# A hybrid decoder block on one core: three made-ahead operand kinds stored unsplit, a final norm computed by positions, and a reordered end

## The chip, the cores and the metric

The kernel runs on one core of one Trainium2 chip. The metric is the device time of one execution in microseconds, taken as the median of several runs.

The five engines have the names that the profile gives them. PE is the matmul engine, and PEld its weight loads. DVE, ACT and POOL are the three elementwise engines. SP issues every DMA of this kernel.

## The reference

One layer of a decoder block on 2048 positions with 1024 channels:

```python
h = rmsnorm(x, norm1_g)
proj = h @ w_in                      # queries, keys, values, gates, conv inputs
o_gla = silu(p_g) * rmsnorm(gated_linear_attention(q, k, v, log_a))
o_conv = c_b * causal_depthwise_conv(c_c * c_h)
x = x + concat(o_gla, o_conv) @ w_out
h2 = rmsnorm(x, norm2_g)
x = x + (silu(h2 @ w_ffn_gate) * (h2 @ w_ffn_up)) @ w_ffn_down
return rmsnorm(x, norm_f_g)
```

`rmsnorm` divides a position's 1024 channels by the root of their mean square plus 1e-6, and multiplies by a gain per channel.

## The kernel before

**Layout.** Activations lie transposed: channels on the 128 partitions, positions along the row. The 2048 positions are four blocks of 512. A half is two blocks (`j` is 0 or 1), and the input projection, the output projection and the feed-forward part each run over half 0 and then half 1.

**Products.** A float32 operand is written as a sum of two reduced-precision (`fp32r`) tiles, `hi` and `lo`, by `split` (lines 145 to 147): ACT copies with rounding (line 146), DVE subtracts (line 147). Each product is three matmuls, hi·hi, hi·lo and lo·hi (lines 359 to 361). A `unit` (line 365 on) multiplies a 2x2 block matrix of weights with a 2x2 block matrix of activations in seven products in place of eight; the activation operands are called, in the order of use, B11, T1, T2, B21, T3, B22 and T4, with four tiles each. A tile of operands holds `hi` beside `lo`, 128 x 1024 words. The pool `opp` has 28 of them.

**Operands made ahead.** While half 0 is multiplied, a generator that is stepped between the products makes the operands of half 1 (`combine`, line 266 on) and puts them into DRAM. `h1_ahead` does so for the input projection: it splits each operand and stores `hi` and `lo` with two DMAs. `h2_ahead` does so for the feed-forward part, through `store_split` (one DMA of 512 KB from a pool of three buffers `so`). When half 1 begins, `load_pairs` and `load_h2` load 28 operands, already split, into `opp`.

**Final norm of half 0.** `finish_later` is stepped while half 1's feed-forward part runs. For each block `j` it sums the squares by channels, and `psum_rstd` (line 167) multiplies the sums by a matrix of ones (line 171), which leaves the total of each position on all partitions, 128 x 512. `finish_rstd` (lines 175 to 180) then makes the inverse root: ACT logarithm (line 177) and exponential (line 178), and DVE steps on 128 x 512 tiles (lines 179 and 156 to 158). Line 975 scales.

**The end.** `last_unit` computes the last two channel tiles of half 1 in four groups of 18 matmuls, in the order (j, r) = (0,0), (0,1), (1,0), (1,1). After each group line 1019 adds on DVE, line 1021 squares on ACT, and line 988 applies the gain on ACT. `norm(0)` stands after the group (1,0), `norm(1)` after (1,1): two matmuls with ones (lines 993 and 994), `finish_rstd`, and a copy of the result for POOL (line 996). `scale` (line 1002) then multiplies the eight tiles of one `j`, six on DVE and two on POOL, and stores each. The built program has on DVE, one after the other, the six scales of j = 0, the last add (line 1019), the norm of j = 1, and its six scales. On PE the group (1,1) follows the two matmuls of `norm(0)` directly.

**What sets the order.** Each engine works off its own list in order. The lists come from a scheduler that simulates the whole program when it is built, so an edit can move instructions far from it; `tc.issue_after(x)` keeps what follows behind `x` in that simulation. A DMA waits in SP's one list until its source or its destination is ready.

Of the kernel before, what the change touches and what calls it, by code (L numbers as in the profile page):

```python
# [10 lines left out]
F32 = mybir.dt.float32  # L11
F32R = mybir.dt.float32r
U32 = mybir.dt.uint32
AF = mybir.ActivationFunctionType
ALU = mybir.AluOpType
PSUM = bass.MemoryType.PSUM
# [2 lines left out]
P = 128  # L19
D = 1024  # L20
SEQ = 2048
PB = 512
NB = SEQ // PB
KD = D // P
PT = PB // P
# [6 lines left out]
EPS = 1e-6  # L32


PRODUCTS = [
    ("A11", "B11"), ("S1", "T1"), ("S2", "T2"), ("A12", "B21"),
    ("S3", "T3"), ("S4", "B22"), ("A22", "T4"),
]
# [2 lines left out]
LATER = ("B21", "T3", "B22", "T4")  # L41


C_G1, C_G2, C_GF, C_BG, C_GN, C_CW = 0, 8, 16, 24, 26, 27
N_SMALL = 39

# [2 lines left out]
def tile_hymba_block(ctx, tc, x, xt, win, wa, wgu, wout, wffn, wdown, wdown_first, small, out):  # L49
    nc = tc.nc  # L50
    act, dve, pool, pe = nc.scalar, nc.vector, nc.gpsimd, nc.tensor

    def pool_of(name, bufs, **kw):
        return ctx.enter_context(tc.tile_pool(name=name, bufs=bufs, **kw))

    const = pool_of("const", 1)
    opp = pool_of("opp", 28)
# [3 lines left out]
    tiny = pool_of("tiny", 2)  # L61
    ps = pool_of("ps", 8, space=PSUM)
    dram = pool_of("dram", 1, space=DRAM)

    mixing = ExitStack()
    mixer = mixing.enter_context(tc.tile_pool(name="mixer", bufs=1))
# [1 line left out]
    bx = [mixing.enter_context(tc.tile_pool(name="bx", bufs=11)), None]  # L68


    ident = mixer.tile([P, P], F32, name="ident")
    make_identity(nc, ident)
    ones = const.tile([P, P], F32, name="ones")
    dve.memset(ones[:], 1.0)
# [3 lines left out]
        out=mask[:], in_=mask[:], compare_op=ALU.is_ge, fill=0.0, base=0,  # L78
        pattern=[[0, 2], [1, P]], channel_multiplier=-1,
    )  # L80
    one_t = ones[:, 0:1]
# [16 lines left out]
    def scratch(name, n):  # L98
# [16 lines left out]
        for half in range(2)  # L115
    ]
    s_h2 = {n: [dram.tile([P, PB], F32, name=f"sf{n}_{k}") for k in range(4)] for n in LATER}
    s_h2p = {
        n: [dram.tile([P, 2, PB], F32, name=f"sh{n}_{k}") for k in range(4)] for _, n in PRODUCTS
    }  # L120
    s_h1 = {
        n: [dram.tile([P, 2, PB], F32, name=f"si{n}_{k}") for k in range(4)] for _, n in PRODUCTS
    }

    def col(c):
# [2 lines left out]
    def bank(name="mm"):  # L128
        return ps.tile([P, PB], F32, name=name, tag="mm")
# [4 lines left out]
    def bt(name, shape=(P, PB)):  # L134
        return bx[0].tile(list(shape), F32, name=name, tag="b")

    def load(dst, src):
        return nc.sync.dma_start(dst, src)

    def store(dst, src):  # L140
        return nc.sync.dma_start(dst, src)

    last_hi, raw_loads = [], []

    def split(src, hi, lo):
        last_hi[:] = [act.activation(hi, src, AF.Copy)]  # L146
        return dve.tensor_tensor(lo, src, hi.bitcast(F32), ALU.subtract)  # L147
# [20 lines left out]
    def psum_rstd(ssq, n):  # L168

        tot, rb = bank("tot"), bank("rb_ps")  # L170
        pe.matmul(tot[:], ones[:], ssq[:], start=True, stop=True)
        finish_rstd(ssq, tot, n, rb)
        return rb

    def finish_rstd(v, tot, n, rb=None):
        l, y0 = bt("l"), bt("y0")
        act.activation(l[:], tot[:], AF.Ln, bias=eps[:], scale=1.0 / n)
        act.activation(y0[:], l[:], AF.Exp, scale=-0.5)
        dve.tensor_scalar(v[:], tot[:], 1.0 / n, EPS, ALU.mult, ALU.add)
        newton((v if rb is None else rb)[:], v[:], l[:], y0[:])  # L180
# [38 lines left out]
    def no_operands():  # L219
        return {b: [] for _, b in PRODUCTS}  # L220
# [233 lines left out]
    rbs, raws, first_weights, last_load, rows, squares = {}, {}, {}, [], {}, {}  # L454
# [54 lines left out]
    def h1_ahead():  # L509

        def put(n, k, h):
            hi, lo = [bx[0].tile([P, PB], F32R, name=e, tag="b") for e in ("hi", "lo")]
            split(h[:], hi[:], lo[:])
            for e, y in enumerate((hi, lo)):
                store(s_h1[n][k][:, e, :], y[:].bitcast(F32))

        yield from combine(lambda k, j: xt[2 + j, :, k, :], C_G1, (rbs[2], rbs[3]), put)

    def load_pairs(src):
        ops = no_operands()  # L520
        for _, n in PRODUCTS:
            ops[n] = [load_pair(p) for p in src[n]]
        return ops

    def load_pair(src):
        o = opp.tile([P, 2, PB], F32R, name="op", tag="op")
        load(o[:].bitcast(F32), src[:])
        return o
# [143 lines left out]
    def gla_scores(b, t, kq, kt, v, g):  # L672
# [174 lines left out]
    def h2_ahead(ssq):  # L847


        rb = []  # L850
        for j in range(2):
            for _ in range(2):
                yield
            rb.append(psum_rstd(ssq[j], D))

        def put(n, k, h):
            store_split(s_h2p[n][k], h)

        yield from combine(lambda k, j: s_x1[2 + j][k][:], C_G2, rb, put)

    def load_h2():
        ops, loads = no_operands(), raw_loads[-2]
        for _, n in PRODUCTS:
            for k in range(4):
                o = opp.tile([P, 2, PB], F32R, name="op", tag="op")
                with tc.issue_after(loads.ins):
                    load(o[:].bitcast(F32), s_h2p[n][k][:])
                ops[n].append(o)
        return ops

# [88 lines left out]
    def finish_later(half):  # L959

        for j in range(2):
            ssq = tiny.tile([P, PB], F32, name="ssx0", tag="ssx0", bufs=1)
            for d in range(KD):
                y = bt("y")
                load(y[:], s_x1[2 * half + j][d][:])
                yield
                sum_squares(ssq, y[:], d == 0)
            yield
            act.preload_act_table_set("natural_log_exp_and_others")
            rb = psum_rstd(ssq, D)  # L970
            for d in range(KD):
                y = bt("y")
                load(y[:], s_x1[2 * half + j][d][:])
                yield
                dve.scalar_tensor_tensor(y[:], y[:], col(C_GF + d), rb[:], ALU.mult, ALU.mult)
                store(out[2 * half + j, :, d, :], y[:])

    def last_unit(src, ops, b12, y, ssq):


        raw = raw_weights(src)
        w = [weight_quarter(raw[:, i, :]) for i in (0, 1, 3, 2)]
        columns = (ops["B11"], ops["B21"]), (b12, ops["B22"])
        with tc.issue_after(last_hi[0].ins):
            act.preload_act_table_set("natural_log_exp_and_others")

        def gain(d, j):
            act.activation(y[d, j], y[d, j], AF.Copy, scale=col(C_GF + d))

        def norm(j, q):  # L990

            tot, rb = bank("tot"), bank("rb")
            pe.matmul(tot[:], ones[:], ssq[j][:], start=True, stop=False)
            pe.matmul(tot[:], ones[:], q[:], start=False, stop=True)
            finish_rstd(ssq[j], tot, D, rb)
            act.activation(ssq[j][:], rb[:], AF.Copy)
            return rb

        def scale(j, rb):
            for d in range(KD):  # L1000
                eng, by = (pool, ssq[j]) if d in (2, 5) else (dve, rb)
                eng.tensor_tensor(y[d, j], y[d, j], by[:], ALU.mult)
                store(out[2 + j, :, d, :], y[d, j])

        for d in range(KD - 2):
            for j in range(2):
                gain(d, j)
        q, rbs = {}, []
        for j in range(2):
            for r in range(2):  # L1010
                o = bank()
                with ExitStack() as stack:
                    if j or r:
                        stack.enter_context(tc.issue_after(done.ins))
                    for i in range(2):
                        for k in range(len(b12)):
                            done = product_step(o, w[2 * r + i], columns[j][i], k, i == 0)
                yy = y[KD - 2 + r, j]
                dve.tensor_tensor(yy, o[:], yy, ALU.add)
                q[j] = tt("q")  # L1020
                act.activation(q[j][:], yy, AF.Square)
                gain(KD - 2 + r, j)
                if not r:
                    pool.tensor_tensor(ssq[j][:], ssq[j][:], q[j][:], ALU.add)
                if j and not r:
                    rbs.append(norm(0, q[0]))
        rbs.append(norm(1, q[1]))
        for j in range(2):
            scale(j, rbs[j])


    act.preload_act_table_set("natural_log_exp_and_others")
# [3 lines left out]
    ops, first, differences = build_h()  # L1036
# [9 lines left out]
    ops = load_pairs(s_h1)  # L1046
# [122 lines left out]
```

## Time and profile before

| What | Value |
|---|---|
| median of 3 runs | 2122.82 us (2122.73 to 2124.79) |
| profiled execution | 2120.33 us |
| its span, first to last instruction | 2118.6 us |
| PE busy share | 96% |
| moved by DMA | 470.74 MB |
| granted matmul clock, mean | 0.989 |

The span is what the views of the trace divide into stages; 1.7 us of the profiled execution lie outside it. In a row of a timeline the first number is the start in microseconds from the span's start and the second the duration; the brackets name how long the engine was idle before and what ended it. In a row of stages each engine has its busy time and its instructions, and PEclk is the granted clock of the matmul engine.

### The profile page before, as it was taken

To read this page: it belongs to the slowest core of one execution; us is meant where nothing else is said; L and a number is where in the kernel's file an instruction comes from. 1 tells how busy PE (TensorE), PEld (TensorE's weight loads), DVE (VectorE), ACT (ScalarE), POOL (GpSimd) and SP (SyncE) were. 2 spreads that over 40 slices of the span, in tenths; PEclk is the share of its full clock that TensorE was granted. 3 is DMA by queue.
4 is the path that set the end of the run, shared out by engine and by line. 5 is a ranking of instruction groups with operands and counts; after the bars stand their busy time and mean duration, and the time that the engine had idled before them with its cause. 6 is when DMAs were issued, how large, how long until landed. Compare 5 with 4: busy or idle time off the path is not lost.

```text
span 2118.6 us, 26920 instructions
## 1 busy us (share of the span) xinstructions
PE 2038.3 (96%) x9133; PEld 1651.9 (78%) x9133; DVE 1412.8 (67%) x1983; ACT 1014.8 (48%) x1997; POOL 973.8 (46%) x703
## 2 busy tenths in 40 slices
PE   6999999999999999999999999999999989999996
PEld 4777787887888887778888878787888878877774
DVE  7668775548754696887887565555776766665554
ACT  5555444656543345544545453333554554543344
POOL 3435322222102364555564348764635544436774
PEclk9999999999999999999999999999999999999998
DMA  7349586433586882655655687697455535587662
GB/s 277 125 150 317 184 328 225 137 110 123 181 310 211 335 286 91 232 220 185 232 190 204 229 331 269 236 340 312 150 206 185 200 138 189 181 345 279 268 268 110
DMA packets 190971, 470.74 MB, mean 222 GB/s; under 512 B 20016, under 2 KB 65264, under 8 KB 181232
## 3 DMA queue, kind: packets, MB, share of 16 engines
q1 hardware_dynamic: 190832, 469.01, 60.8%
q8 instruction: 72, 1.18, 0.2%
q14 instruction: 67, 0.55, 0.1%
HBM read 300.63 MB, written 168.30 MB: 221 GB/s over the span
## 4 chain that ended last, share of the span: by engine, by line
PE 78%; DVE 8%; DMA 6%; issue 3%; ACT 2%; POOL 2%; SPq 0%; DVEq 0%; ACTq 0%; POOLq 0%
PE mm L359 22%; PE mm L361 22%; PE mm L360 22%; PE mm L777 2%; PE mm L778 2%; PE mm L780 2%; DVE wq L147 2%; DVE so L147 1%; DMA op<-shT 1%; DMA raw<-in_wffn_dram 1%; DMA raw<-in_wdown_dram 1%; PE a_ps L541 1%; DVE op L147 1%; ACT wq L146 1%; DMA raw<-in_win_dram 1%
## 5 line engine op out<-in xcount | busy, mean ns | idle before, releaser
L359 PE MATMUL mm<-op,wq 128*128 128x512 f32 x2499 | 983.0, 395 | 27.0 <-ACT c L379 10.7
L361 PE MATMUL mm<-op,wq 128*128 128x512 f32 x2499 | 968.3, 393 | 15.2 <-DVE wq L147 14.2
L360 PE MATMUL mm<-op,wq 128*128 128x512 f32 x2499 | 977.6, 391 | 0.0
L147 DVE TENSOR_TENSOR wq<-raw,wq 128x512 fp32r<-128x512 f32 (+2 forms) x626 | 523.3, 843 | 338.6 <-ACT wq L146 336.3
L146 ACT ACTIVATE wq<-raw 128x512 fp32r<-128x512 f32 (+2 forms) x626 | 363.9, 587 | 563.1 <-PE mm L361 407.0
L359 PEld LDWEIGHTS mm<-op,wq 128*128 128x128 f32 x2499 | 471.7, 189 | 141.8 <-ACT c L379 14.8
L361 PEld LDWEIGHTS mm<-op,wq 128*128 128x128 f32 x2499 | 471.5, 189 | 127.9 <-DVE wq L147 29.0
L360 PEld LDWEIGHTS mm<-op,wq 128*128 128x128 f32 x2499 | 472.0, 189 | 97.2 <-issue 1.0
L344 POOL TENSOR_TENSOR raw<-s,raw 128x512 f32<-128x512 f32 (+2 forms) x97 | 128.3, 1323 | 441.7 <-DVE wq L147 421.6
L383 DVE TENSOR_TENSOR c<-mm,c 128x512 f32<-128x512 f32 x267 | 182.9, 685 | 98.4 <-PE mm L361 94.7
L342 POOL TENSOR_TENSOR s<-raw 128x512 f32<-128x512 f32 (+2 forms) x97 | 130.0, 1340 | 206.7 <-DMA raw<-in_wffn_dram 84.8
L349 POOL TENSOR_TENSOR raw<-raw 128x512 f32<-128x512 f32 (+2 forms) x97 | 125.1, 1290 | 139.6 <-DVE wq L147 132.4
L379 ACT ACTIVATE c<-mm 128x512 f32<-128x512 f32 x267 | 154.7, 585 | 39.8 <-PE mm L361 37.4
L759 POOL TENSOR_TENSOR ssx<-ssx,q 128x512 f32<-128x512 f32 x52 | 76.1, 1476 | 155.4 <-ACT q L758 155.2
L343 POOL TENSOR_TENSOR raw<-raw 128x512 f32<-128x512 f32 (+2 forms) x97 | 137.4, 1416 | 4.1
L948 POOL TENSOR_TENSOR y<-c,y 128x512 f32<-128x512 f32 x66 | 98.7, 1498 | 49.0 <-DVE c L383 48.7
L147 DVE TENSOR_TENSOR so<-t,so 128x512 fp32r<-128x512 f32 x100 | 91.0, 916 | 23.6 <-ACT so L146 23.0
L146 ACT ACTIVATE wq<-s 128x512 fp32r<-128x512 f32 (+2 forms) x97 | 56.8, 586 | 95.4 <-PE mm L361 88.6
L777 PE MATMUL mm<-op,wq 128*128 128x512 f32 x256 | 100.9, 395 | 0.0
L778 PE MATMUL mm<-op,wq 128*128 128x512 f32 x256 | 99.8, 390 | 0.0
L147 DVE TENSOR_TENSOR wq<-s,wq 128x512 fp32r<-128x512 f32 (+2 forms) x97 | 85.0, 876 | 15.7 <-ACT wq L146 15.1
L146 ACT ACTIVATE so<-t 128x512 fp32r<-128x512 f32 x100 | 62.3, 626 | 39.2 <-DMA sa_B<-so 14.6
(175 smaller groups left out, 1884.4 us busy)
## 6 DMA issues: line engine op xcount, KB each, us to landing
raw<-in_wffn_dram SPq DMA_DIRECT2D x44, 1024.0 KB, 5.5
sa_T<-so SPq DMA_DIRECT2D x88, 512.0 KB, 5.0
op<-sa_T SPq DMA_DIRECT2D x88, 512.0 KB, 8.7
sa_B<-so SPq DMA_DIRECT2D x69, 512.0 KB, 3.4
op<-sa_B SPq DMA_DIRECT2D x69, 512.0 KB, 9.1
raw<-in_win_dram SPq DMA_DIRECT2D x23, 1024.0 KB, 5.3
raw<-in_wdown_dram SPq DMA_DIRECT2D x24, 768.0 KB, 6.2
sx<-y SPq DMA_DIRECT2D x48, 256.0 KB, 3.2
```

Source lines behind the costliest of these rows:

```text
L146: last_hi[:] = [act.activation(hi, src, AF.Copy)]
L147: return dve.tensor_tensor(lo, src, hi.bitcast(F32), ALU.subtract)
L342: pool.tensor_tensor(s1, a21, a22, ALU.add)
L343: pool.tensor_tensor(a21, a11, a21, ALU.subtract)
L344: pool.tensor_tensor(a11, s1, a11, ALU.subtract)
L359: pe.matmul(o[:], wh, xh, start=first and k == 0, stop=False, skip_group_check=True)
L360: pe.matmul(o[:], wh, xl, start=False, stop=False, skip_group_check=True)
L361: return pe.matmul(o[:], wl, xh, start=False, stop=k == n - 1, skip_group_check=True)
L379: act.activation(t[:], o[:], AF.Copy)
L383: dve.tensor_tensor(t[:], o[:], t[:], ALU.add)
L777: pe.matmul(o[e, j][:], wh, m[:, 0, :], start=k == 0, stop=False)
L778: pe.matmul(o[e, j][:], wh, m[:, 1, :], start=False, stop=False)
```

## The change

1. **Stored whole.** T3, B22 and T4 (12 of the 28 operands) are stored by `h1_ahead` and by `h2_ahead` as they are, 256 KB each, without a split. `load_whole` loads such an operand into the second half of its `opp` tile and splits it there, so ACT's copy and DVE's subtraction are done at the loading.
2. **The norm by positions.** `position_rstd` replaces the norm in `finish_later` and in `last_unit`. The squares are the stationary side of matmuls with one column of ones, four (or eight) per block, so the totals stand as 128 x 4: one position on each partition. DVE alone makes the inverse root, from an integer first guess and three Newton steps: twelve instructions on 128 x 4 tiles. A copy spreads it to 128 x 512, and four transposes put it on all partitions; in `last_unit` four more write a second copy for ACT and POOL. `ident` moves to the pool that lives to the end, and the loads of ACT's function table in `finish_later` and `last_unit` go.
3. **The end.** The last add (line 1019) goes ahead of the scales of j = 0. POOL scales three tiles of j = 0 (2, 5, 6); DVE scales tiles 0 and 1 behind the last add, and tiles 3, 4 and 7 behind the copy `rep` of `norm(1)`.

```diff
+WHOLE = ("T3", "B22", "T4")
...
+    def position_rstd(n, *sums, into=()):
+        s, rb = bank("rs"), bank("rb_ps")
+        tot, v, l = [s[:, i * PT : (i + 1) * PT] for i in range(3)]
+        y = tiny.tile([P, PT], F32, name="py", tag="py")[:]
+        for t in range(PT):
+            for i, ssq in enumerate(sums):
+                pe.matmul(
+                    tot[:, t : t + 1], ssq[:, t * P : (t + 1) * P], one_t, start=i == 0,
+                    stop=i == len(sums) - 1,
+                )
+        dve.tensor_scalar(v, tot, 1.0 / n, EPS, ALU.mult, ALU.add)
+        li = l.bitcast(I32)
+        dve.tensor_scalar(li, v.bitcast(I32), 1, None, ALU.arith_shift_right)
+        dve.tensor_scalar(y.bitcast(I32), li, -1, 0x5F3759DF, ALU.mult, ALU.add)
+        for _ in range(3):
+            dve.tensor_tensor(l, v, y, ALU.mult)
+            dve.scalar_tensor_tensor(l, l, -0.5, y, ALU.mult, ALU.mult)
+            dve.scalar_tensor_tensor(y, l, 1.5, y, ALU.add, ALU.mult)
+        rep = bt("rep", (P, PT, P))
+        last_rep[:] = [
+            dve.tensor_copy(rep[:], y.rearrange("p (t c) -> p t c", c=1).to_broadcast([P, PT, P]))
+        ]
+        for dst in (rb, *into):
+            for t in range(PT):
+                pe.transpose(dst[:, t * P : (t + 1) * P], rep[:, t, :], ident[:])
+        return rb
...
         def put(n, k, h):
+            if n in WHOLE:
+                store(s_h1[n][k][:], h[:])
+                return
...
+    def load_whole(src):
+        o = opp.tile([P, 2, PB], F32R, name="op", tag="op")
+        load(o[:, 1, :].bitcast(F32), src[:])
+        split(o[:, 1, :].bitcast(F32), o[:, 0, :], o[:, 1, :])
+        return o
...
         def put(n, k, h):
-            store_split(s_h2p[n][k], h)
+            if n in WHOLE:
+                store(s_h2p[n][k][:], h[:])
+            else:
+                store_split(s_h2p[n][k], h)
...
-            act.preload_act_table_set("natural_log_exp_and_others")
-            rb = psum_rstd(ssq, D)
+            rb = position_rstd(D, ssq)
...
-            tot, rb = bank("tot"), bank("rb")
-            pe.matmul(tot[:], ones[:], ssq[j][:], start=True, stop=False)
-            pe.matmul(tot[:], ones[:], q[:], start=False, stop=True)
-            finish_rstd(ssq[j], tot, D, rb)
-            act.activation(ssq[j][:], rb[:], AF.Copy)
+            copied = bank("rb_ps")
+            rb = position_rstd(D, ssq[j], q, into=[copied])
+            act.activation(ssq[j][:], copied[:], AF.Copy)
             return rb
...
                 if j and not r:
-                    rbs.append(norm(0, q[0]))
-        rbs.append(norm(1, q[1]))
-        for j in range(2):
-            scale(j, rbs[j])
+                    rb = norm(0, q[0])
+                    for d in (2, 5, 6):
+                        scale(0, d, None)
+        for d in (0, 1):
+            with tc.issue_after(added.ins):
+                scale(0, d, rb)
+        rb1 = norm(1, q[1])
+        for d in (3, 4, 7):
+            with tc.issue_after(last_rep[0].ins):
+                scale(0, d, rb)
+        for d in range(KD):
+            scale(1, d, None if d in (2, 5) else rb1)
```

In the built program of the changed kernel, PE has the eight column matmuls and the eight transposes of `norm(0)` ahead of the 18 matmuls of the group (1,1). On DVE the last add follows the copy `rep` of `norm(0)`, then two scales, the chain of `norm(1)`, three scales of j = 0, and the six of j = 1. In `finish_later`, 24 matmuls stand on PE between the last column matmul and the first transpose for the first block, and 12 for the second. At the start of each half 1, the twelve splits of `load_whole` stand in the lists of ACT and DVE among the weight splits of the first two units.

More of the change, by code (lines that the diff above doesn't have):

```diff
@@ L13 @@
 U32 = mybir.dt.uint32
+I32 = mybir.dt.int32
 AF = mybir.ActivationFunctionType
@@ L68, in tile_hymba_block @@
     bx = [mixing.enter_context(tc.tile_pool(name="bx", bufs=11)), None]
-    ident = mixer.tile([P, P], F32, name="ident")
+    ident = const.tile([P, P], F32, name="ident")
     make_identity(nc, ident)
@@ L117, in tile_hymba_block, with made_ahead @@
     s_h2 = {n: [dram.tile([P, PB], F32, name=f"sf{n}_{k}") for k in range(4)] for n in LATER}
+    def made_ahead(name, n):
+        return dram.tile([P, PB] if n in WHOLE else [P, 2, PB], F32, name=name)
     s_h2p = {
-        n: [dram.tile([P, 2, PB], F32, name=f"sh{n}_{k}") for k in range(4)] for _, n in PRODUCTS
+        n: [made_ahead(f"sh{n}_{k}", n) for k in range(4)] for _, n in PRODUCTS
     }
     s_h1 = {
-        n: [dram.tile([P, 2, PB], F32, name=f"si{n}_{k}") for k in range(4)] for _, n in PRODUCTS
+        n: [made_ahead(f"si{n}_{k}", n) for k in range(4)] for _, n in PRODUCTS
     }
@@ L173, in psum_rstd @@
         return rb
+    def position_rstd(n, *sums, into=()):
[24 more added lines that the diff above has]
+        return rb
+    last_rep = []
     def finish_rstd(v, tot, n, rb=None):
@@ L521, in load_pairs @@
         for _, n in PRODUCTS:
-            ops[n] = [load_pair(p) for p in src[n]]
+            ops[n] = [(load_whole if n in WHOLE else load_pair)(p) for p in src[n]]
         return ops
+    def load_whole(src):
[3 more added lines that the diff above has]
+        return o
     def load_pair(src):
@@ L864, in load_h2 @@
             for k in range(4):
-                o = opp.tile([P, 2, PB], F32R, name="op", tag="op")
                 with tc.issue_after(loads.ins):
-                    load(o[:].bitcast(F32), s_h2p[n][k][:])
+                    o = (load_whole if n in WHOLE else load_pair)(s_h2p[n][k])
                 ops[n].append(o)
@@ L983, in last_unit @@
         columns = (ops["B11"], ops["B21"]), (b12, ops["B22"])
-        with tc.issue_after(last_hi[0].ins):
-            act.preload_act_table_set("natural_log_exp_and_others")
         def gain(d, j):
@@ L990, in norm, with scale @@
         def norm(j, q):
-            tot, rb = bank("tot"), bank("rb")
-            pe.matmul(tot[:], ones[:], ssq[j][:], start=True, stop=False)
-            pe.matmul(tot[:], ones[:], q[:], start=False, stop=True)
-            finish_rstd(ssq[j], tot, D, rb)
-            act.activation(ssq[j][:], rb[:], AF.Copy)
-            return rb
[L999 to L1003, printed above, removed]
+            copied = bank("rb_ps")
+            rb = position_rstd(D, ssq[j], q, into=[copied])
+            act.activation(ssq[j][:], copied[:], AF.Copy)
+            return rb
+        def scale(j, d, rb):
+            eng, by = (dve, rb) if rb is not None else (pool, ssq[j])
+            eng.tensor_tensor(y[d, j], y[d, j], by[:], ALU.mult)
+            store(out[2 + j, :, d, :], y[d, j])
         for d in range(KD - 2):
@@ L1007, in last_unit @@
                 gain(d, j)
-        q, rbs = {}, []
+        q = {}
         for j in range(2):
@@ L1018, in last_unit @@
                 yy = y[KD - 2 + r, j]
-                dve.tensor_tensor(yy, o[:], yy, ALU.add)
+                added = dve.tensor_tensor(yy, o[:], yy, ALU.add)
                 q[j] = tt("q")
```

## Prediction

> **What bounds the kernel now.** I read the page first, then the table of waits, then the stages, and last the timeline at the places that the change touches.
>
> ```profile
> PE 2038.3 (96%) x9133; PEld 1651.9 (78%) x9133; DVE 1412.8 (67%) x1983; ACT 1014.8 (48%) x1997; POOL 973.8 (46%) x703
> PE 78%; DVE 8%; DMA 6%; issue 3%; ACT 2%; POOL 2%; SPq 0%; DVEq 0%; ACTq 0%; POOLq 0%
> PE mm L361 <- DVE wq L147: 14.2, 11, 2.5
> ```
>
> The matmuls are the bound, and the change leaves every product in place. So only PE's stalls can be won: it is idle for 2118.6 - 2038.3 = 80 us. The third row is the largest of its waits: 14.2 us in 11 pieces, for DVE's half of a weight split. The stages that the change touches:
>
> ```profile
> 130.00:250.00 120.00, 110.42 (x457) 86.32 (x456) 109.02 (x147) 67.52 (x127) 57.96 (x36) 0.97 0.75 256
> 300.00:340.00 40.00, 38.31 (x196) 30.75 (x194) 22.06 (x41) 19.19 (x52) 9.68 (x8) 1.00 0.90 331
> 840.00:1040.00 200.00, 194.60 (x848) 158.20 (x848) 163.28 (x194) 106.34 (x185) 109.64 (x73) 1.00 0.57 210
> 1425.00:1475.00 50.00, 46.48 (x194) 37.04 (x193) 22.59 (x29) 18.82 (x33) 19.91 (x15) 0.97 0.89 348
> 1720.00:1740.00 20.00, 12.95 (x48) 9.88 (x47) 13.94 (x20) 12.34 (x19) 5.80 (x4) 0.83 0.69 254
> ```
>
> The columns behind the stage's length are PE, PEld, DVE, ACT, POOL, the granted clock, DMA's share and GB/s. Row one is the stage of h1_ahead: DVE is busy 109 of 120 us, and PE loses 9.6 us idle and 0.03 x 120 = 3.6 us by a slower clock. Row three is h2_ahead, where PE loses 5.4 us. Rows two and four are the starts of the two second halves: DMA is at 0.9, DVE has room, and PE loses 1.7 us and 3.5 + 1.5 us. Row five is the second norm of finish_later: 7 us idle and 3.4 us of slow clock. A stall costs more than itself:
>
> ```profile
> 246.09 0.50 PE L359 MATMUL mm<-op,wq 128*128 128x512 f32 x1 [2.08 <-ACT c L379]
> 247.36 0.63 PE L361 MATMUL mm<-op,wq 128*128 128x512 f32 x1
> 250.77 0.39 PE L360 MATMUL mm<-op,wq 128*128 128x512 f32 x1
> ```
>
> After 2.08 us of idleness, eight matmuls from 247.36 to 250.77 start 0.43 us apart (3.41 / 8); the five from 246.09 take 1.27 us, 0.25 each. Eight times the 0.18 between is 1.4; with what the first five lost I put 1.6 us on such a stall.
>
> *The Trainium skill, "TensorE: Matmul & The Clock Gate", section "What's actually happening", has the clock halve after an idle window of about 3.4 us. The trace disagrees: 2.08 us were enough here.*
>
> **The change part by part.** Six terms, in us of the profiled execution; minus is faster.
>
> ```profile
> L147 DVE TENSOR_TENSOR so<-t,so 128x512 fp32r<-128x512 f32 x100 | 91.0, 916 | 23.6 <-ACT so L146 23.0
> L147 DVE TENSOR_TENSOR lo<-h,hi 128x512 fp32r<-128x512 f32 x16 | 15.5, 971 | 0.1
> L146 ACT ACTIVATE hi<-h 128x512 fp32r<-128x512 f32 x16 | 9.9, 625 | 4.8 <-DMA siB<-hi 2.6 <-DMA siT<-hi 1.5 <-POOL h L254 0.6
> op<-shT SPq DMA_DIRECT2D x16, 512.0 KB, 9.2
> sx<-y SPq DMA_DIRECT2D x48, 256.0 KB, 3.2
> ```
>
> *A, h1_ahead: -4.* Twelve splits go: DVE sheds 12 x 0.97 = 11.6 us, ACT 12 x 0.63 = 7.5, and SP issues 12 stores less. DVE was free for 11 us in this stage and is now free for 22. Its waits end on DVE, so they should shrink, but several come from one instruction that stands in front, not from the average. I take a third of PE's 13.2 us. Ends: -8 (nearly two thirds) and +1 (the lists are scheduled anew here, and a new order can stall in another place).
>
> *B, start of half 1 of the projection: +1.* The 12 splits come back: DVE has 22 of 40 us busy, ACT 19, and they become 33 and 27. What hides it is DVE's room and operands that are loaded early. If that cover is gone, the weight splits queued behind a split whose load is late come late for PE. Half the loaded bytes of 12 operands go, 3 MB, which at 331 GB/s is 9 us of DMA. Ends: -1 and +5.
>
> *C, h2_ahead: -2.* The same 12 splits go, by the `so` row 12 x 0.92 = 11 us of 163 on DVE in 200. The norm inside this stage stays, and part of the 5.4 us is its. Ends: -4 and +1.
>
> *D, start of half 1 of the feed-forward part: -2.*
>
> ```profile
> 1447.30 8.80 DMA sx<-y
> 1456.12 9.95 DMA op<-shT
> ```
>
> This is the chain of waits: the last tile of T4 needs its place in `opp`, which a store frees after 8.80 us, and then loads for 9.95, far over the median of 3.2 us of such a store, because DMA is full. With 3 MB less in the stage both get shorter; 4 us less would end PE's loss of 5. But T3, B22 and T4 must now be split after landing: 0.63 on ACT and 0.7 to 0.97 on DVE ahead of PE's use. Ends: -5 and +3.
>
> *The Trainium skill, "DMA: Bandwidth & Descriptors", in its fit for one DMA, has 2.0 us plus the bytes by 436 GB/s. By it half an operand saves only 0.6 us of its landing and D would be about +1; the fit is for a queue that is free, and the rows above show this one full.*
>
> *E, finish_later: -2.5.*
>
> ```profile
> 1729.39 1.28 ACT L177 ACT_TABLE_LOAD   x1
> 1730.69 0.69 ACT L177 ACTIVATE l<-tot,eps 128x512 f32<-128x512 f32 x1
> 1731.28 0.62 ACT L146 ACTIVATE so<-t 128x512 fp32r<-128x512 f32 x1
> 1731.91 1.28 ACT L178 ACT_TABLE_LOAD   x1
> 1733.21 0.63 ACT L178 ACTIVATE y<-l 128x512 f32<-128x512 f32 x1
> 1734.48 0.68 DVE L383 TENSOR_TENSOR c<-mm,c 128x512 f32<-128x512 f32 x1
> 1735.22 0.80 PE L359 MATMUL mm<-op,wq 128*128 128x512 f32 x1 [7.05 <-DVE c L383]
> ```
>
> PE waits from 1728.2 to 1735.2 for an addition that stands on DVE behind the norm, and the norm waits for two table loads and two functions on ACT, 3.9 us. These go. What is late next is the `so` split, whose buffer waits for a store: I put ACT's copy at 1729.4 and the addition at 1730.7, so PE goes on at 1731.3, 3.9 us earlier, still after a stall long enough for the slow clock. Then the column matmuls and transposes interrupt PE, and the first block's norm, which cost no stall before, pays them too: together about 1.4 us. Covered by 24 and 12 matmuls, the chain on DVE costs PE nothing if it starts in time. Ends: -6 (no stall at all) and +2 (the transposes wait for a chain behind late splits).
>
> *F, the end: +3.5.*
>
> ```profile
> 13.14 0.16 DVE L157 SCALAR_TENSOR_TENSOR rl<-rl,msq 128x4 f32<-128x4 f32 x1
> 13.34 0.16 DVE L158 SCALAR_TENSOR_TENSOR msq<-rl,ry 128x4 f32<-128x4 f32 x1
> L450 DVE COPY rep<-msq 128x128 f32<-128x128 f32 x16 | 3.7, 266 | 6.5 <-PE rb_ps L451 6.5
> 303.96 0.89 PE o_ps L701 x8
> 13.90 1.45 PE L451 MATMUL rb_ps<-ident,rep 128*128 128x128 f32 x4 [13.90 <-DVE rep L450]
> 2092.23 1.02 PE L993 MATMUL tot<-ssx,ones 128*128 128x512 f32 x2
> 2093.55 0.79 PE L359 MATMUL mm<-op,wq 128*128 128x512 f32 x1
> 2098.07 1.02 PE L993 MATMUL tot<-ssx,ones 128*128 128x512 f32 x2
> 2098.64 3.68 DVE L1002 TENSOR_TENSOR y<-y,rb 128x512 f32<-128x512 f32 x6 [0.66 <-ACT ssx L996]
> 2102.23 0.68 DVE L1019 TENSOR_TENSOR y<-mm,y 128x512 f32<-128x512 f32 x1
> 2109.42 3.68 DVE L1002 TENSOR_TENSOR y<-y,rb 128x512 f32<-128x512 f32 x6 [0.66 <-ACT ssx L996]
> ```
>
> Before, the last group ran from 2093.55 to 2098.07, 4.5 us; its add waited for six scales until 2102.23; the scales of j = 1 began 7.19 us after it. After, PE must pass `norm(0)` before the last group. The column matmuls are not in the trace. A float32 matmul is recorded twice (L993), so eight are 16 passes; the nearest row is o_ps with 0.11 a pass, which gives 1.8; a quarter of its columns' work would give half of that, and I take 1.5. DVE's chain is 12 steps 0.20 apart (13.14 to 13.34), 2.4. The copy `rep` has four times the elements of a row that takes 0.27; between that and the 0.68 of a full tile (L383) I take 0.5. Eight transposes take 0.9 at 0.11 and 2.9 at the 0.36 of the slow row (1.45 / 4); I take 1.5. With 0.5 of handovers PE reaches the last group 6.4 us behind 2092.2; its 4.5 us gain 1.6 of slow clock, since PE sat idle for 3.4. The last add comes at 2092.2 + 6.4 + 6.1 + 0.2 = 2104.9 in place of 2102.2: +2.7. From there to the scales of j = 1: add 0.7, square 0.65, columns 1.5, chain 2.4, copy 0.5, handovers 0.4, and three scales of 0.61 that hide the transposes, 8.0 in place of 7.2: +0.8. Six scales and the stores follow as before. Ends: -1 (warm clock, columns at 0.05) and +7 (all at the slow rate).
>
> *Sum*: -4 + 1 - 2 - 2 - 2.5 + 3.5 = -6.0, so 2120.3 - 6.0 = 2114.3 for an execution like the profiled one. The median of the runs lies 2.5 us above that execution; the difference goes onto the median: 2122.8 - 6.0 = **2116.8**.
>
> **The rivals.**
>
> *The late split, slower than before.* Place: the first unit of each half 1. PE uses up an operand in three matmuls, about 0.7 us by the five starts above; DVE's `so` splits take 0.92 on the average, and it has weight splits and additions besides. If T3 lands no earlier than now, the last three products, 8 us of PE, need 12 x 0.92 + 7 x 0.8 = 16.6 us of DVE, 8 us more for each of the two starts. For: landing took 9.2 us at the median, so operands arrive late. Against: ACT and DVE were half idle in both stages, and the loads are halved. B and D with +6 each in place of -1 together give +7: 2129.8. It turns the sign from the point where both together cost over 5 us.
>
> *The relief buys nothing.* In A and C PE's waits may end on one particular instruction that a freer DVE reaches no sooner. With A and C at 0, and E at -2.5 against F at +3.5, the sum is 0: 2122.8. For: DVE is at 0.82 in C and PE loses little there. Against: the largest wait in the table is for DVE.
>
> *More than that.* A at -8, D at -4, F at +1, the rest as above: -13.5, so 2109.3. For F: by the clock rule that I cited no slow clock would follow, and F would be 1.6 smaller; the trace speaks against it. That the end does not do what its name says is no separate case: F already has the last add later than before.
>
> **How the numbers follow.** Forecast 0.5, nothing 0.22, more 0.14, late split 0.14. Taken half-way and by squares, the ends of the six terms give about 9 us to each side of the forecast: 2108 to 2126; that leaves out most of the late split and the far end of "more", some 0.2 in all. A change of 0.2%, 4.2 us, is about what a measurement of this kernel can tell from none. The forecast's own range, 2112 to 2121, crosses that bound, so of its 0.5 I count 0.44 as faster and 0.06 as the same: faster 0.44 + 0.14 + 0.02 of the second rival's spread = 0.60; same 0.25; slower 0.15.
>
> **What would show it.** For A, DVE's busy time in 130 to 250 falls by about 10 us and PE's rises by 2 to 5; wrong if PE stays at 110. For B and D, waits of PE or PEld for `op` splits on DVE would show the late split; D is right if the last wait for shT is gone. For E, no table loads at the second norm, and a stall of 3 instead of 7 us. For F, PE idle about 3 us between column matmuls and transposes, slow starts after them, and the last add 10 us or more ahead of the first scale of j = 1 would be worse than I said. The prediction is wrong as a whole if the new order of the lists costs PE stalls in stages that no part of the change touches.

## The result and the profile after

| What | Predicted | Measured |
|---|---|---|
| median of 6 runs, changed kernel | 2116.8 us (2108 to 2126) | 2107.21 us (2101.95 to 2108.46) |
| median of 6 runs, kernel before, same chip | | 2123.11 us (2121.15 to 2127.50) |
| ratio | 0.9972 | 0.9922, 95% interval 0.9909 to 0.9934 |
| profiled execution, span | | 2106.52 us, 2104.4 us |

The direction was right and the size was not: by the ratio the change wins 16.6 us (14.0 to 19.3), not 6, and the time lies just below the range. The two profiled executions differ by 14.2 us of span.

First the page of the changed kernel and its table of waits, the rows that answer to the first three of before:

```profile
PE 2036.8 (97%) x9193; PEld 1656.3 (79%) x9193; DVE 1415.8 (67%) x2018; ACT 998.6 (47%) x1982; POOL 973.1 (46%) x704
PE 72%; DVE 7%; DMA 6%; issue 3%; ACT 2%; POOL 2%; SPq 1%; DVEq 0%; ACTq 0%; POOLq 0%
PE mm L401 <- DVE wq L155: 10.0, 7, 2.5
```

These rows would not have told it. DVE's busy time went *up* by 3 us, and the wait for weight splits fell by 4.2 us in all. (Line 361 of before is line 401 here, 147 is 155, 359 is 399, 379 is 419, 383 is 423, 1019 is 1064, 1002 is 1047.)

The products are the same in both kernels and in the same order, so I counted them: product matmul number n does the same work in both, and the difference of its two starts is what the kernel has won up to there. What each stretch adds to that difference, in us of the profiled executions (times of before):

| Stretch | What the change does there | Predicted | Measured |
|---|---|---|---|
| start to 125 | nothing | 0 | -1.7 |
| 125 to 253 | A, `h1_ahead` | -4 | **-11.4** |
| 253 to 350 | B, half 1 of the projection begins | +1 | -1.4 |
| 350 to 836 | nothing | 0 | +0.4 |
| 836 to 1258 | C, `h2_ahead` | -2 | +0.4 |
| 1423 to 1484 | D, half 1 of the feed-forward part begins | -2 | -2.5 |
| 1511 to 1767 | E, `finish_later` | -2.5 | -4.7 |
| 1876 to 2089 | nothing | 0 | +4.1 |
| 2089 to the end | F | +3.5 | +2.6 |
| all | | -6.0 | -14.2 |

One stretch, A, is 7.4 of the 8.2 us that were missed. The stages of the changed kernel that answer to the five rows of before, each set earlier by what has been won up to there (1.7 to 15 us). The first is the stretch A of the table above:

```profile
123.50:240.00 116.50, 113.37 (x486) 90.02 (x485) 106.15 (x144) 66.18 (x124) 59.09 (x38) 1.00 0.75 252
287.00:327.00 40.00, 40.00 (x214) 32.19 (x214) 33.12 (x58) 26.15 (x68) 10.16 (x8) 1.00 0.74 259
826.00:1026.00 200.00, 195.34 (x847) 159.47 (x846) 158.76 (x186) 101.50 (x177) 109.23 (x73) 0.99 0.57 204
1411.00:1461.00 50.00, 47.33 (x205) 37.97 (x205) 33.87 (x44) 25.82 (x46) 22.21 (x16) 1.00 0.77 290
1705.00:1725.00 20.00, 17.85 (x84) 14.58 (x83) 15.30 (x31) 10.05 (x19) 6.69 (x5) 1.00 0.70 263
```

The same matmuls of the first row in before:

```profile
125.20:253.10 127.90, 118.32 (x486) 91.96 (x485) 114.11 (x156) 72.54 (x136) 59.78 (x38) 0.97 0.73 248
```

The same matmuls take 116.5 us in place of 127.9, at full clock. PE is idle for 3.1 us and not 9.6, and DVE has 12 instructions and 8.0 us of work less. Row two shows the splits come back at the start of half 1 (DVE 33 instead of 22 us, ACT 26 instead of 19, as forecast) with PE busy for all 40 us: DVE had the room, and DMA fell from 331 to 259 GB/s. In row three PE gains only 0.7 us although DVE and ACT each do nearly 5 us less. In row five PE's loss of 7 us has become 2.

### The profile page after: what moved, and what is told of

Its sections match the earlier page's. It is cut to its first block, busy times and chain, and to the rows that moved or that the text cites. A ratio compares the mean times of both kernels' runs of the same rounds, so it can differ in the third digit from the quotient of the medians.

```text
span 2104.4 us, 27023 instructions
## 1 busy us (share of the span) xinstructions
PE 2036.8 (97%) x9193; PEld 1656.3 (79%) x9193; DVE 1415.8 (67%) x2018; ACT 998.6 (47%) x1982; POOL 973.1 (46%) x704
## 4 chain that ended last, share of the span: by engine, by line
PE 72%; DVE 7%; DMA 6%; issue 3%; ACT 2%; POOL 2%; SPq 1%; DVEq 0%; ACTq 0%; POOLq 0%
PE mm L399 20%; PE mm L401 20%; PE mm L400 20%; PE mm L827 3%; PE mm L828 2%; PE mm L830 2%; DVE wq L155 2%; DVE so L155 1%; DMA raw<-in_wdown_dram 1%; DMA op<-sa_T 1%; DMA x<-sx 1%; POOL y L1000 1%; ACT wq L154 1%; DMA sa_T<-so 1%; PE o_ps L751 1%
## 5 line engine op out<-in xcount | busy, mean ns | idle before, releaser
L399 PE MATMUL mm<-op,wq 128*128 128x512 f32 x2499 | 980.7, 394 | 20.1 <-ACT wq L154 8.4
L400 PE MATMUL mm<-op,wq 128*128 128x512 f32 x2499 | 975.8, 391 | 0.7 <-DVE op L155 0.7
L401 PE MATMUL mm<-op,wq 128*128 128x512 f32 x2499 | 965.5, 392 | 10.7 <-DVE wq L155 10.0
L827 PE MATMUL mm<-op,wq 128*128 128x512 f32 x256 | 100.9, 395 | 0.0
L828 PE MATMUL mm<-op,wq 128*128 128x512 f32 x256 | 99.7, 389 | 0.0
L155 DVE TENSOR_TENSOR wq<-s,wq 128x512 fp32r<-128x512 f32 (+2 forms) x97 | 79.9, 823 | 15.1 <-ACT wq L154 14.5
L830 PE MATMUL mm<-op,wq 128*128 128x512 f32 x256 | 79.8, 390 | 0.0
```

What stands on the lines that cost most here:

```text
L399: pe.matmul(o[:], wh, xh, start=first and k == 0, stop=False, skip_group_check=True)
L400: pe.matmul(o[:], wh, xl, start=False, stop=False, skip_group_check=True)
L401: return pe.matmul(o[:], wl, xh, start=False, stop=k == n - 1, skip_group_check=True)
L827: pe.matmul(o[e, j][:], wh, m[:, 0, :], start=k == 0, stop=False)
L828: pe.matmul(o[e, j][:], wh, m[:, 1, :], start=False, stop=False)
```

## The experiments

All times are compared with runs of the kernel before on the same chip, taken with them (medians of 2123.61, 2124.65 and 2124.09 us in the three groups). "Stage A" is the difference by the count of products against before, from 125 to 253 us.

### Each part alone

The change in four parts, each on the kernel before: only `h1_ahead` stores whole; only `h2_ahead` does; only `finish_later` has the norm by positions; only `last_unit` is changed.

```diff
+            if n in WHOLE:                  # s1_h1, in h1_ahead
+                store(s_h1[n][k][:], h[:])
...
+            if n in WHOLE:                  # s2_h2, in h2_ahead
+                store(s_h2p[n][k][:], h[:])
...
-            rb = psum_rstd(ssq, D)          # s3_norm, in finish_later
+            rb = position_rstd(D, ssq)
```

> Only the projection's T3, B22 and T4 stored whole. Theory, DVE is the bound of the stage of h1_ahead and work taken from it counts one for one: -12 us (about -11 in the stage 130 to 250, -1 at the start of half 1). Rival, the forecast's sizes: -3 us (-4 and +1). Rival, the gain comes from a new order of the lists elsewhere: the stage 130 to 250 keeps at least 8 us of PE's loss.

> Only the feed-forward part's T3, B22 and T4 stored whole. Theory, DVE has room while h2_ahead runs, so only the start of half 1 gains: -2.5 us, and nothing between 840 and 1240. Rival, the forecast's sizes: -4 us, half of it between 840 and 1040.

> Only the norms of finish_later by positions. Theory, the stall at the second norm is the two table loads and two functions on ACT: -5 us, and no idle time of PE over 2 us there. Rival, the stall is the store that frees a split's buffer: -2.5 us or less, 3 us idle left.

> Only the end: norms of last_unit by positions and the new order. Theory, PE waits about 3 us for the copy of norm(0) ahead of the last group, and the last group starts 6.5 us later than before: +2.6 us in all. Rival, the earlier last add wins more than that wait costs: -3 us.

| Alone | Median | Ratio, 95% interval | By the count of products |
|---|---|---|---|
| `h1_ahead` | 2110.66 us | 0.9940 (0.9924 to 0.9957) | A -11.3, B -1.3 |
| `h2_ahead` | 2122.87 us | 0.9998 (0.9987 to 1.0009) | C -0.2 up to 1091 and +3.0 from there to 1258, D -3.3 |
| `finish_later` | 2119.79 us | 0.9988 (0.9975 to 1.0001) | E -3.8 |
| `last_unit` | 2127.39 us | 1.0016 (1.0004 to 1.0028) | F +2.1 |

The first part alone brings 12.7 of the 16.6 us; the four ratios add up to 12.3, and the rest is within their intervals. The second and third gain in their places but not measurably in the time. The end by itself is slower: its last group starts 5.3 us later and what follows is 3.2 us shorter.

### Which resource of `h1_ahead`: DVE, ACT or the stores

Twelve splits less are three things less: DVE's subtractions, ACT's copies, and 12 stores of 256 KB. Each was put back into the changed kernel by itself, ahead of the whole stores: a `max` of the tile with itself on DVE, a copy in place on ACT, or a second store.

```diff
             if n in WHOLE:
+                dve.tensor_tensor(h[:], h[:], h[:], ALU.max)   # a1_dve
+                act.activation(h[:], h[:], AF.Copy)            # a2_act
+                store(s_again[n][k][:], h[:])                  # a3_store
                 store(s_h1[n][k][:], h[:])
```

> The changed kernel, with one DVE instruction more (the larger of a tile and itself, 128 x 512, in place) ahead of each of the twelve whole stores of h1_ahead: 12 x 0.69 = 8.3 us of DVE come back, no ACT work and no DMA. Theory, DVE is the bound of that stage: +7 us against the changed kernel, all of it between 125 and 253. Rivals, ACT's rounding copies or the stores were the bound: +1 us at most.

> The changed kernel, with one ACT copy in place, 128 x 512, ahead of each of the twelve whole stores of h1_ahead: 12 x 0.63 = 7.5 us of ACT come back. Theory, DVE is the bound: 0 to +1 us against the changed kernel. Rival, ACT's rounding copies were the bound: +6 us between 125 and 253.

> The changed kernel, with each of the twelve whole operands of h1_ahead stored a second time, to a tensor that nothing reads: the 12 DMAs and 3 MB that the change took out of the stage come back. Theory, DVE is the bound: 0 to +1 us against the changed kernel. Rival, the stores, their buffers or SP's list were the bound: +5 us between 125 and 253.

| Put back | Median | Ratio, 95% interval | Stage A | Given back of 11.4 |
|---|---|---|---|---|
| nothing (the changed kernel) | 2107.21 us | 0.9922 (0.9909 to 0.9934) | -11.4 | |
| 12 on DVE | 2115.14 us | 0.9961 (0.9944 to 0.9978) | -3.1 | 8.3 |
| 12 on ACT | 2110.57 us | 0.9933 (0.9914 to 0.9953) | -11.4 | 0.0 |
| 12 stores | 2113.26 us | 0.9948 (0.9932 to 0.9965) | -8.3 | 3.1 |

DVE's work is most of it, ACT's none. The stores cost more than I had allowed: they count for a part. Each of these edits also gave the scheduler a new order on DVE; with ACT's copies the order changed too and stage A did not, so a new order alone is not seen to cost this. How the stores act is suggested by one group of DVE in 125 to 250 us, first of the changed kernel and then of the one with the second stores:

```profile
L155 DVE TENSOR_TENSOR lo<-h,hi 128x512 fp32r<-128x512 f32 x8 | 10.4, 1301 | 1.0 <-ACT hi L154 0.8
```

```profile
L157 DVE TENSOR_TENSOR lo<-h,hi 128x512 fp32r<-128x512 f32 x8 | 11.8, 1476 | 1.7 <-DMA siT<-hi 0.8 <-ACT hi L156 0.8
```

DVE now waits for a store to free a tile (`siT<-hi`, behind the bar), and the same eight subtractions take longer. That the stores act through DVE too fits these rows, but it is not shown by a run of its own. That DVE's and the stores' parts add up to 11.4 is not more than their sum: the two together were not tried.

The waits of PE in 125 to 250 us, for before, the changed kernel, DVE's work put back, and ACT's put back:

```profile
PE mm L361 <- DVE wq L147: 5.3, 4, 2.1
PE mm L359 <- ACT c L379: 4.0, 3, 2.1
```

```profile
PE mm L401 <- DVE wq L155: 2.1, 1, 2.1
PE mm L399 <- ACT c L419: 0.9, 1, 0.9
```

```profile
PE mm L401 <- DVE wq L155: 5.2, 4, 2.1
PE mm L399 <- DVE c L423: 1.5, 2, 1.2
PE mm L399 <- ACT c L419: 1.2, 2, 0.9
```

```profile
PE mm L401 <- DVE wq L155: 2.1, 1, 2.1
```

9.3 us of waits became 3.0, with DVE's work 7.9 again, with ACT's 2.1. The row that names ACT (4.0 us for `c`) shrank to 0.9 as DVE's load fell and is gone with ACT's work back. At the longest of these waits in before, ACT's copy stands behind another that had waited for DVE, so the last releaser's name was not the cause there:

```profile
244.93 0.63 ACT L146 ACTIVATE hi<-c 128x512 fp32r<-128x512 f32 x1 [1.12 <-DVE c L625]
245.46 1.07 ACT L379 ACTIVATE c<-mm 128x512 f32<-128x512 f32 x2
```

### One operand kind in place of three

```diff
-WHOLE = ("T3", "B22", "T4")
+WHOLE = ("T4",)
```

On the kernel before, in `h1_ahead` alone: four splits go in place of twelve.

> The kernel before, with T4 alone stored whole by h1_ahead: four splits leave the stage in place of twelve, 3.9 us of DVE. Theory, DVE's work counts one for one while the stage is bound by it: -4 us in the stage 125 to 253. Rival, a threshold or one particular instruction in front: 0 or already -10.

Stage A: -4.2, which is 1.05 per split beside 0.95 (11.4 / 12) with twelve. But the time went *up*: 2127.46 us, ratio 1.0017 (1.0002 to 1.0031). By the count the profiled execution loses 6.1 us between 314 and 350 us, at the start of half 1. The timeline there:

```profile
326.39 0.81 ACT L707 ACTIVATE carry<-state,em 64x128 f32<-64x128 f32 x2 [1.58 <-DVE state L733]
327.02 0.50 PE L364 MATMUL mm<-op,wq 128*128 128x512 f32 x1 [0.60 <-DVE op L151]
331.26 1.06 ACT L383 ACTIVATE c<-mm 128x512 f32<-128x512 f32 x2
331.89 0.79 PE L363 MATMUL mm<-op,wq 128*128 128x512 f32 x1 [4.14 <-ACT c L383]
```

The late split of my rival is there, in the second row: 0.6 us. The 4.14 us are for another thing, a copy on ACT that frees a bank and stands behind the copies of the attention's `state`, which wait for DVE. The long duration (0.79) in the last row marks the slow clock after it. With three times as many returning splits the changed kernel has no such wait (its row 287 to 327 above). So the loss does not go with the number of splits. That it goes with the order of this kernel's lists is likely but not tested.

### The end: the transposes behind the last group, and the old end

First, in the changed kernel, `norm(0)` is cut in two: the column matmuls and DVE's chain stay, and the transposes go behind the last group's 18 matmuls. Second, the changed kernel with the `last_unit` of before.

```diff
-                    rb = norm(0, q[0])
-                    for d in (2, 5, 6):
-                        scale(0, d, None)
+                    copied = bank("rb_ps")
+                    *banks, rep0 = position_chain(D, ssq[0], q[0], into=[copied])
+        with tc.issue_after(done.ins):
+            rb = spread(rep0, banks)
+        act.activation(ssq[0][:], copied[:], AF.Copy)
+        for d in (2, 5, 6):
+            scale(0, d, None)
```

> The changed kernel with one move on PE: the transposes of the first block's norm at the end stand behind the last group's 18 matmuls, so that those fill the time in which DVE makes the inverse root. In the changed kernel PE waits 2.9 us for the copy rep there and the last group starts 6.6 us later than before. If that wait and the slow clock behind it are what the end costs (my theory), the last group comes 4 to 5 us earlier and the whole is 3 to 5 us faster than the changed kernel (2102 to 2104 if that is at 2107). Rival: the end is set by DVE's list (the last add, two scales, the second norm's chain), and the transposes' wait only moves behind the group: 0 to -1.

> The changed kernel with the end of before (the norm of the last unit by the matrix of ones and ACT, six scales of j = 0 ahead of nothing new); only the ends of the lists differ from the changed kernel. With the end alone on the kernel before, the time went up by 2 to 3.4 us. If that price is the same here, this one is 2.6 to 3.4 us faster than the changed kernel and the profile has the last group 5 to 7 us earlier and what follows it 3 to 4 us longer. Rival: the price seen there was jitter of the rounds, then 0 +- 1.

| Version | Median of 5 | Ratio, 95% interval | From 2089 us of before to the end |
|---|---|---|---|
| changed kernel | 2107.21 us (6 runs) | 0.9922 (0.9909 to 0.9934) | +2.6 |
| transposes behind | 2104.94 us | 0.9909 (0.9893 to 0.9925) | **-3.0** |
| old end | 2104.93 us | 0.9898 (0.9880 to 0.9916) | -0.2 |

In the traces the move is worth 5.6 us, more than I had said, and the old end 2.8. The times point the same way, by 2.8 and 5.1 us at the ratios, but the intervals of the three overlap. The old end and the one with the transposes behind have the same median, so no time here shows a gain of the new end over the old one. The timelines at the place, the changed kernel and then the one with the transposes behind:

```profile
2075.61 0.69 DVE L1064 TENSOR_TENSOR y<-mm,y 128x512 f32<-128x512 f32 x1 [3.40 <-PE mm L401]
2080.20 1.97 PE L210 MATMUL rb_ps<-ident,rep 128*128 128x128 f32 x8 [2.94 <-DVE rep L206]
2088.03 0.69 DVE L1064 TENSOR_TENSOR y<-mm,y 128x512 f32<-128x512 f32 x1 [7.89 <-PE mm L401]
2094.10 1.97 PE L210 MATMUL rb_ps<-ident,rep 128*128 128x128 f32 x8 [2.94 <-DVE rep L206]
```

```profile
2078.91 0.69 DVE L1071 TENSOR_TENSOR y<-mm,y 128x512 f32<-128x512 f32 x1 [3.40 <-PE mm L408]
2084.81 0.69 DVE L1071 TENSOR_TENSOR y<-mm,y 128x512 f32<-128x512 f32 x1 [0.47 <-PE mm L408]
2085.89 1.09 PE L217 MATMUL rb_ps<-ident,rep 128*128 128x128 f32 x8 [1.12 <-DVE rep L210]
```

The last add comes 5.9 us after the add before it, in place of 12.4. PE waits 1.1 us and not 2.9, and its clock stays up.

This run also says how sure the count of products is. The two kernels have the same lists up to the last group, yet against each other they drift by +2.1 (682 to 794 us), +1.6 (883 to 967) and -3.1 (1944 to 1975), and by 0.1 in all from 123 to 335. A single step of 1 to 3 us elsewhere can thus be one execution's. Stage A's is not: it is -11.3 with `h1_ahead` alone, -11.5 with the transposes behind and -11.4 with the old end.

## Why the prediction was right or wrong

**A failed, in its size.** The step is "I take a third of PE's 13.2 us", with the reason that several waits "come from one instruction that stands in front, not from the average". All 11.4 us were won. The average that I read, DVE busy 109 of 120 us, held the answer and I drew the wrong thing from it: 11 us free in 120 is not 11 us free anywhere. Cut finer, the kernel before:

```profile
207.00:247.00 40.00, 35.05 (x147) 26.77 (x146) 39.79 (x50) 18.98 (x38) 18.05 (x12) 1.00 0.68 226
```

DVE has 0.2 us of idle time in 40, and PE loses 5 there and more by the slow clock that follows. In such a stretch every DVE instruction moves all that is behind it, whichever of them PE's waits happen to name. Of the 11.4 us, 8.2 were won from 207 us on. The other 3 were won between 160 and 207, where DVE is busy about 0.8 of the time, so a full piece is not the whole account.

The runs put two terms in the place of the third. DVE's twelve instructions are worth about 8.3, which came back with twelve `max` in their place, and the stores, to which the prediction gave no time, 3.1; a third of both would be 3.8, and four splits less gave 4.2. The 12 x 0.97 = 11.6 that the prediction has DVE shed is near 11.4 by luck: it holds no stores, and DVE's busy time for the same matmuls fell by 8.0 only. With the twelve `max` back it rose by 8.7, though these took 1.24 us each, 14.8 in all. In this stage an instruction that takes 0.69 by itself was worth about 0.69, even where its own row shows more; the last section shows what goes with the rest.

**B was too careful**: -1.4, by one's own part -1.3. The cover that I named held (the row 287 to 327). The late split was priced at 8 us for each start; the largest wait for a late split seen is 0.7 us, in D:

```profile
PE mm L400 <- DVE op L155: 0.7, 1, 0.7
PE mm L399 <- ACT op L154: 0.3, 1, 0.3
```

**C was wrong**: nothing. For the same matmuls (836 to 1258) DVE and ACT each have 7.3 us of work less, but where PE did not wait. The other kernels with this `h2_ahead` were 0.6 to 3.3 us slower here, and those with the old one between 0.0 and 2.0 slower, so neither a gain nor a loss is shown. PE's longest wait there is the same before and after, for the weight split behind a `so` split (before, then after):

```profile
857.31 0.63 ACT L146 ACTIVATE so<-t 128x512 fp32r<-128x512 f32 x1 [2.81 <-POOL t L247]
858.65 0.63 ACT L146 ACTIVATE so<-t 128x512 fp32r<-128x512 f32 x1 [0.19 <-DMA sa_B<-so]
860.16 0.50 PE L361 MATMUL mm<-op,wq 128*128 128x512 f32 x1 [2.51 <-DVE wq L147]
```

```profile
843.19 0.63 ACT L154 ACTIVATE so<-t 128x512 fp32r<-128x512 f32 x1 [2.83 <-POOL t L287]
844.62 0.63 ACT L154 ACTIVATE so<-t 128x512 fp32r<-128x512 f32 x1 [0.27 <-DMA sa_B<-so]
846.04 0.50 PE L401 MATMUL mm<-op,wq 128*128 128x512 f32 x1 [2.54 <-DVE wq L155]
```

ACT waits for POOL, DVE stands behind ACT, PE behind DVE. Here the rival "the relief buys nothing" was right, at DVE 0.82; at 0.99 it was wrong.

**D was right**: -2.5 (-3.6 at the place), and -2.6 to -3.3 in the six other kernels with it. PE's wait for `shT` is gone. The landings of the window 1380 to 1480 us of the changed kernel:

```profile
op<-shT SPq DMA_DIRECT2D x8, 512.0 KB, 9.4
op<-shT SPq DMA_DIRECT2D x8, 256.0 KB, 7.9
```

*By the fit of the Trainium skill, "DMA: Bandwidth & Descriptors", section "Anatomy of one DMA — SWDGE (gpsimd) path", that I had cited, half an operand saves 0.6 us, with 3.2 and 2.6 for the two sizes by my estimate from it. That fit is for DMAs issued from GpSimd, and SP issues these; nor does it say that it is for a queue that is free, as I had put it; the medians here differ by 1.5, and both lie far above it.*

**E had the right mechanism and was too small**: -4.7 for -2.5, and -3.3 to -3.9 in the six other kernels with this norm. No table load is left. The stall that I put at 3 us is 1.9 in all seven. In this execution the clock stays up behind it:

```profile
1715.10 0.50 PE L399 MATMUL mm<-op,wq 128*128 128x512 f32 x1 [1.90 <-DVE c L423]
1718.35 0.66 PE L210 MATMUL rb_ps<-ident,rep 128*128 128x128 f32 x4 [0.25 <-DVE rep L206]
```

With `finish_later` alone it does not, and matmuls follow 0.43 us apart, as I had expected (the last two rows are three matmuls apart):

```profile
1732.69 0.50 PE L392 MATMUL mm<-op,wq 128*128 128x512 f32 x1 [1.94 <-DVE c L416]
1733.58 0.63 PE L392 MATMUL mm<-op,wq 128*128 128x512 f32 x1
1734.86 0.63 PE L392 MATMUL mm<-op,wq 128*128 128x512 f32 x1
```

The slow clock followed in four of the seven; in two of the others the transposes waited 1.3 us for `rep` instead. So about 1 us of the -4.7 is this execution's. Here the second norm gives 6.2 net and the first takes 1.3; I had 3.9 to gain, and 1.4 to pay for both.

**F was right in its steps, and near in their sizes.** The add of the group (1,0) in before, then the first and the last step of DVE's work for `norm(0)` and, from the chain that ended last, the columns in the changed kernel:

```profile
2092.43 0.69 DVE L1019 TENSOR_TENSOR y<-mm,y 128x512 f32<-128x512 f32 x1 [3.39 <-PE mm L361]
```

```profile
2077.30 0.17 DVE L196 TENSOR_SCALAR rs<-rs 128x4 f32<-128x4 f32 x1 [0.99 <-PE rs L192]
...
2079.71 0.43 DVE L206 COPY rep<-py 128x512 f32<-128x512 f32 x1
```

```profile
2075.58 1.69 PE rs L192 x16
```

The last add came 2102.23 - 2092.43 = 9.8 us after the add before it and now comes 12.4 after it: +2.6 (predicted 2.7). The columns, for which I had no row, take 1.7 (1.5), DVE's twelve steps 2.41 (2.4), the copy 0.43 (0.5), eight transposes 1.97 (1.5); the whole end costs 2.6 (3.5), since the part behind the last add is a little shorter than I had it. That the slow clock cost the last group 1.5 us (1.6) has luck in it: behind the same stall of 2.94 us it cost 0.2, 0.3, 0.9 and 1.5 in the four other kernels with this order of the end.

**Untouched stages.** 1876 to 2089 us costs 4.1, which no step had. Of that, 1.9 between 1920 and 1955 belongs to the change: such a stall in an untouched stage is what the prediction had named as the sign of being wrong as a whole. It stands in all seven kernels with the new `finish_later` (1.5 to 1.9) and in none of the four without, as a new wait for a weight split; how the norm's edit led to it was not traced. In the changed kernel:

```profile
1929.73 0.50 PE L399 MATMUL mm<-op,wq 128*128 128x512 f32 x1 [1.75 <-ACT wq L154]
```

Another 3.0 is a late load. The kernel with the transposes behind has the same lists there and does not lose it; only the one with ACT's copies back lost as much (3.2). Between 2040 and 2060, 1.6 come back. The rows of the late load:

```profile
1964.83 1.00 POOL L382 TENSOR_TENSOR s<-raw 128x384 f32<-128x384 f32 x1 [3.66 <-DMA raw<-in_wdown_dram]
1965.44 0.51 PE L399 MATMUL mm<-op,wq 128*128 128x512 f32 x1 [1.50 <-ACT wq L154]
```

The 1.7 us before 125 are of the same kind: the ten other kernels lie between -2.8 and +1.6 there. That the profile of after is 0.7 us below its median, and that of before 2.8 us, makes the difference of the medians larger than that of the spans.

**The rivals.** One sum of the prediction is off: the sizes of "more than that" add up to -14.5 and not -13.5, which is 2108.3 us. It came nearest to the measured time, but in part by luck: A was larger than even its -8, and its D and F were further off than the forecast's.

## What to carry to other kernels

Before you price work taken from an engine, cut the stage until the engine's idle time in a piece is nothing or clearly something: where DVE was nearly always full, twelve instructions less brought most of 11.4 us, and where it was busy 0.82 of the time twelve less brought nothing. Price an instruction by what it takes undisturbed, and the stores that go with it by themselves. The engine that the waits name is the last in line and not always the cause; put the suspected work back alone and see which part of the gain leaves. And where the bound engine must wait for a short chain, move what waits behind the next block of its work: in the traces the same transposes cost 5.6 us less behind 18 matmuls than ahead of them.

## What the runs showed of the hardware

After a stall of 2.94 us the clock was slow again. The eight transposes behind it take 1.97 us, 0.25 each, and behind a stall of 1.12 us they take 1.09, 0.14 each. The stage that follows the first, in the changed kernel:

```profile
2080.00:2088.00 8.00, 7.80 (x28) 6.59 (x28) 0.14 (x1) 0.60 (x1) 3.75 (x3) 0.64 0.23 87
```

Right ahead of that stall stand the 1.7 us of column matmuls, which have one column each. If the clock counts those as idle, it saw 4.6 us of it; this row does not say how short a stall is enough. At the second norm of `finish_later` the same stall of 1.9 us was followed by the slow clock in four kernels and not in three, so its length alone does not decide it.

*The Trainium skill, "TensorE: Matmul & The Clock Gate", section "What's actually happening", has the clock go down after at least one idle window of about 3.4 us. This place agrees with it if the columns count as idle; the 2.08 us in the prediction, behind full matmuls, do not.*

DVE's busy time is not a fixed cost per instruction. The subtraction `lo<-h,hi` took 0.97 us on the average in before (16 of them), 1.30 in the changed kernel (the 8 that are left) and 1.48 with more stores beside it, all on tiles of the same size. What goes with the longer ones is POOL. Of the 807 subtractions of 128x512 tiles with a `fp32r` result in before, 470 ran with no POOL instruction beside them in the trace and took 0.66 to 0.70 us; all 219 that took more than 0.8, up to 1.83, overlapped one. No run changed POOL's work, so this is what the trace shows together and not a tested cause.
